# Feed-forward stages: the hidden units computed with the tokens stationary, taken two at a time

## Chip, core and metric

One core of one Trainium2 chip runs the whole program. The metric is the device time of one execution in microseconds (us), as the median of several runs. The profile is a single execution with the hardware profiler on. Engines are named as the profile names them: PE is the matrix engine (PEld its weight load, which overlaps PE), DVE the vector engine, ACT the scalar engine, POOL the GpSimd engine, SP the engine that issues most DMAs.

## What is computed

256 tokens of 1024 channels go through three macaron blocks: feed forward, mixer, feed forward. The kernel runs nine stages in the order f0, m0, f1, f2, m1, f3, f4, m2, f5. The change is in the six feed-forward stages, whose mathematics is this, with 1024 channels, 2816 hidden channels and a residual weight of one half:

```python
def rms_norm_2(x, gain):
    xf = x.astype(jnp.float32)
    y = xf * lax.rsqrt(jnp.mean(xf * xf, axis=-1, keepdims=True) + RMS_EPS)
    return (y * gain.astype(jnp.float32)).astype(x.dtype)

def swiglu_2(x, w_gate, w_up, w_down):
    return (jax.nn.silu(x @ w_gate) * (x @ w_up)) @ w_down

x = x + FFN_RESIDUAL_WEIGHT * swiglu_2(rms_norm_2(x, ffn1_norm[l]),
                                       ffn1_w_gate[l], ffn1_w_up[l], ffn1_w_down[l])
```

## The kernel before

**Precision.** Every float32 factor is split into a high and a low part that PE can multiply fast (type fp32r), and a product is the sum of three: high by high, high by low, low by high. `mm3` (line 176) issues these three matmuls, at lines 177, 178 and 179.

**Weights.** The host lays all weights out as blocks of 128 partitions by 2048 columns in the order of `block_plan`. `W` (line 129) loads a block on first use: two DMAs of 512 KB on SP's queue into `raw` tiles (3 buffers), and for each 512 columns a cast on ACT into `hi` (line 167) and a subtraction on DVE into `lo` (line 169). A block is thus four casts and four subtractions. The pool of split blocks has four buffers, so a block can be split only once the block four before it, or another that is done with, has been used for the last time. The framework orders each engine's instructions by program order and by its own estimate of when they can run; each engine then executes its queue strictly in that order.

**A feed-forward stage** (`ffn`, line 354) has 22 hidden units of 128 channels and two token tiles t = 0, 1 of 128 tokens. The normalized, transposed tokens lie in `xt` as high and low parts.

- `g_as(u, t)` (line 377) computes gate and up of one unit for one token tile with the tokens stationary and the unit's weights moving: for each of 8 slices of the channels one `mm3` with 256 moving columns (128 gate, 128 up). It uses one of the two PSUM banks of `psG`. `glu` (line 363) then reads that bank with three instructions: a tanh `th` on ACT (line 365), `sg` (line 367) and `hu` (line 369) on DVE. The bank is free again when `hu` has run. The result has tokens on partitions, so `g_tr` (line 390) transposes it on PE (line 393) and splits it into `hidh` and `hidl` (lines 182 and 183).
- `g_ws(u)` (line 397) computes a unit for both token tiles with the weights stationary and the tokens moving: per half and channel slice a matmul of 512 columns (line 404) and one of 256 (line 405). Its result needs no transpose.
- `down(u, t)` (line 414) multiplies a unit's hidden channels by its rows of the down weights: six matmuls of 512 columns into two accumulators.

Three units at the head of a stage (four in f4, where `late` is not empty) and two at its tail go through `g_as`, the others through `g_ws`. At the head that lets work on token tile 0 begin while token tile 1 is still being normalized: its last two steps, transposes of the normalized tile at line 224, are hooked into the `g_as` named in line 433, before channel slices 3 and 6, and work on tile 1 comes after. At the tail, `after` (line 278) adds the accumulator of tile 0 to the residual and starts the next stage's norm (`norm_to`, line 227: the scaled tile `xn` is written at line 233, or at line 315 for f4) while PE still works on tile 1. The order at head and tail is written out by hand:

```python
seq = [(u, t) for t in range(NT) for u in range(NA)]     # NA = 3, in f4 4
for i, ut in enumerate(seq):
    hook = finish_at(3, 6) if si and i == NA - 1 else lambda k: None
    g_as(*ut, hook)
    if i > 1:
        g_tr(*seq[i - 2])
...
down(a - 2, 0)                                            # a, b = 20, 21
g_as(a, 0); down(a - 1, 0); g_as(b, 0); g_tr(a, 0); g_as(a, 1); g_tr(b, 0); down(a, 0); down(b, 0)
fin = after(si, 0, acc[0], 0.5)
g_as(b, 1); g_tr(a, 1)
...
down(a - 2, 1); down(a - 1, 1); g_tr(b, 1)
fin()
down(a, 1)
down(b, 1)
```

In f0, `g_as` for token tile 0 runs its three products in three passes over the channels (line 383), since the weights arrive piece by piece.

Of the kernel before, what the change touches and what calls it, by code (L numbers as in the profile page):

```python
# [10 lines left out]
F32R = mybir.dt.float32r  # L11
# [6 lines left out]
P = 128  # L18
D = 1024
KD = 8  # L20
NT = 2
NFU = 22
HALF = 512
EPS = 1e-6
PIECE = 512
# [22 lines left out]
def block_plan(stages):  # L48
    plan = []
    for s in stages:  # L50
        if s[0] == "f":
            for u in range(NFU):
                plan.append(((s, "g", u), 2048))
            for j in range(NFU // 2):
                plan.append(((s, "d", j), 2048))
        elif s == "m0":
            for u in range(4):
                for kh in range(2):
                    plan.append(((s, "p", u, kh), 4 * EV_U))
            for j in range(2):  # L60
                plan.append(((s, "qk", j), 2048))
            for j in range(4):
                plan.append(((s, "o", j), 2048))
        elif s == "m1":
            for kh in range(2):
                plan.append(((s, "a", 0, kh), 4 * IDX_A))
            for u in range(3):
                for kh in range(2):
                    plan.append(((s, "p", u, kh), 2048))
            for j in range(4):  # L70
                plan.append(((s, "o", j), 2048))
# [19 lines left out]
def macaron_kernel(ctx, tc, stages, x, wstream, gains, consts, mconsts, pos, e_small, e_gw, e_on,  # L91
# [95 lines left out]
    def tsl(t):  # L187
        return slice(t * P, (t + 1) * P)
# [165 lines left out]
    def ffn(si):  # L354
        st = stages[si]
        xt = xt_of(si)
        prepare(si + 1)
        fp = ctx2.enter_context(tc.tile_pool(name=f"ffn{si}", bufs=2, reuse_waits="tile"))
        if stages[si:si + 2] == ("f3", "f4"):
            nexts[si + 1]["final"] = load_gain(FINAL_ROW, finp, "fgain")  # L360
        hh, acc, cnt, pend = {}, {}, {(t, n): 0 for t in range(NT) for n in range(2)}, {}

        def glu(ps_g, ps_u, n):
            th = T(fp, 256, "th")
            act(th[:, :n], ps_g, AF.Tanh, scale=0.5)  # L365
            sg = T(fp, 256, "sg")
            V.scalar_tensor_tensor(sg[:, :n], th[:, :n], 1.0, ps_g, op0=ALU.add, op1=ALU.mult)
            hu = T(fp, 256, "hu", bufs=3)
            V.scalar_tensor_tensor(hu[:, :n], sg[:, :n], 0.5, ps_u, op0=ALU.mult, op1=ALU.mult)  # L369
            return hu  # L370

        def hid(u):
            if u not in hh:
                hh[u] = [T(fp, NT * P, f"hid{a}", F32R, bufs=5) for a in "hl"]
            return hh[u]

        def g_as(u, t, hook=lambda k: None):
            wh, wl = W3((st, "g", u), 8, 256)
            ps = bank(psG)
            if si == 0 and t == 0:  # L380
                for i, (a, b) in enumerate(((xt[0], wh), (xt[1], wh), (xt[0], wl))):
                    for k in range(KD):
                        mm(ps[:, :256], lhsT=a[:, k, tsl(t)], rhs=b[:, k], start=i == k == 0, stop=i == 2 and k == 7)  # L383
            else:
                for k in range(KD):
                    hook(k)
                    mm3(ps[:, :256], xt[0][:, k, tsl(t)], xt[1][:, k, tsl(t)], wh[:, k], wl[:, k], k == 0, k == 7)
            pend[u, t] = glu(ps[:, :P], ps[:, P:256], P)

        def g_tr(u, t):  # L390
            hu = pend.pop((u, t))
            pt = bank(psT)
            pe_t(pt[:, :P], hu[:, :P], ident)
            hi, lo = hid(u)
            split_to(hi[:, tsl(t)], lo[:, tsl(t)], pt[:, :P])

        def g_ws(u):
            wh, wl = W3((st, "g", u), 8, 256)
            gu = []
            for m in range(2):  # L400

                ps = bank(psG)
                for k in range(KD):
                    mm(ps, lhsT=wh[:, k, tsl(m)], rhs=xt[2][:, k], start=k == 0, stop=False)  # L404
                    mm(ps[:, :256], lhsT=wl[:, k, tsl(m)], rhs=xt[0][:, k], start=False, stop=k == 7)  # L405
                half = T(fp, 256, "half")
                nc.scalar.copy(half, ps[:, 256:])  # L407
                gu.append(T(fp, 256, f"gu{m}"))
                V.tensor_tensor(gu[m], ps[:, :256], half, op=ALU.add)  # L409
            hu = glu(gu[0], gu[1], 256)  # L410
            hi, lo = hid(u)
            split_to(hi, lo, hu)

        def down(u, t, half=(0, 1)):
            if t not in acc:
                acc[t] = [bank(psA) for _ in range(2)]
            wh, wl = W3((st, "d", u // 2), 2, D)
            a, b = [z[:, tsl(t)] for z in hh[u]]
            for n in half:
                sl = slice(n * HALF, (n + 1) * HALF)  # L420
                mm3(acc[t][n], a, b, wh[:, u % 2, sl], wl[:, u % 2, sl], cnt[t, n] == 0, cnt[t, n] == NFU - 1)
                cnt[t, n] += 1

        if si == 0:
            seq = ((0, 0), (1, 0), (0, 1), (1, 1), (2, 0), (2, 1))
            W((st, "g", 1), (1,))
            W((st, "g", 2), (1, 3), fp)
        else:
            NA = 4 if late else 3
            seq = [(u, t) for t in range(NT) for u in range(NA)]  # L430
        NA = len(seq) // 2
        for i, ut in enumerate(seq):
            hook = finish_at(3, 6) if si and i == NA - 1 else lambda k: None
            g_as(*ut, hook)
            if i > 1:
                g_tr(*seq[i - 2])
        down(0, 0)
        g_tr(*seq[-2])
        down(0, 1)
        g_tr(*seq[-1])  # L440
        a, b = NFU - 2, NFU - 1
        if NA == 4:
            down(1, 0)
            down(1, 1)
        for u in range(NA, a):
            g_ws(u)
            if u == 8:
                with ExitStack() as order:
                    for m in front():
                        order.enter_context(tc.issue_after(m))  # L450
                    while late:
                        late.pop(0)()
                    if st == "f1":
                        rotary_tables()
            down(u - 2, 0)
            if u - 2 < NFU - 4:
                down(u - 2, 1)
        down(a - 2, 0)
        g_as(a, 0); down(a - 1, 0); g_as(b, 0); g_tr(a, 0); g_as(a, 1); g_tr(b, 0); down(a, 0); down(b, 0)
        fin = after(si, 0, acc[0], 0.5)  # L460
        g_as(b, 1); g_tr(a, 1)
        if si + 1 == len(stages):
            for n in range(2):
                for u in (a - 2, a - 1, a, b):
                    if u == a and n == 0:
                        g_tr(b, 1)
                    down(u, 1, (n,))
            after(si, 1, acc[1], 0.5)
            return
        down(a - 2, 1); down(a - 1, 1); g_tr(b, 1)  # L470
        fin()
        down(a, 1)
        down(b, 1)
        tail.append(after(si, 1, acc[1], 0.5))
# [817 lines left out]
    norm_to(0, nexts[0]["gain"], xt_of(0))()  # L1292
    if stages[0][0] == "f":
        with tc.issue_after(last["xn"].ins), tc.issue_after(last["split"].ins):
            W((stages[0], "g", 0), (1,))
    for s in range(2):
        nc.sync.dma_start(h[1][:, s * HALF:(s + 1) * HALF], x[tsl(1), s * HALF:(s + 1) * HALF])
    if stages[0][0] == "f":
# [64 lines left out]
def arrange(inp, stages):  # L1363
# [87 lines left out]
```

## Time and profile before

| | |
|---|---|
| median of 3 runs | 1542.37 us (1540.57 to 1542.55) |
| the profiled execution, its own time | 1545.25 us |
| span of the profile | 1543.5 us |
| mean granted PE clock | 0.993 of full speed |
| PE busy | 1499.1 us, 97% of the span, 8620 matmuls |
| DVE, ACT, POOL busy | 68%, 55%, 7% |
| share of PE on the chain that ended last | 79% |

The chain is followed back from the last instruction through whatever released each step. Matmuls are pipelined, and the profile models their ends, so a row's duration says little of what a matmul costs in a stream; the distance from the start of one to the start of the next does. A number in brackets behind a row of the timeline is the time for which the engine stood idle before it, with the instruction that ended the wait.

### The profile page before, as it was taken

What the parts mean: (1) busy time and instruction counts of PE and PEld (TensorE: products, weight loads), DVE (VectorE), ACT (ScalarE), POOL (GpSimd) and SP (SyncE); (2) the same over time, 40 slices, a digit from 0 to 9 for tenths busy, and PEclk for the clock granted to TensorE, in tenths of its full rate; (3) what the DMA queues carried; (4) which work ended last, traced back from release to release, by engine and by line L of the source; (5) the groups of instructions that cost most, each with busy time, mean ns of one, the idle gap of its engine ahead of it and who ended that gap; (6) DMA issues with size and microseconds to landing.
All of it is one profiled execution on the core that took longest, in us unless ns stands there. A gap on an engine that the chain in (4) does not pass through costs nothing.

```text
span 1543.5 us, 23721 instructions
## 1 busy us (share of the span) xinstructions
PE 1499.1 (97%) x8620; PEld 1308.5 (85%) x8620; DVE 1053.6 (68%) x2282; ACT 851.2 (55%) x1912; POOL 101.3 (7%) x110
## 2 busy tenths in 40 slices
PE   6999998999999999999899999999999999999998
PEld 6888888788888888888688888888888898888887
DVE  6666678766766666668866666767667557776664
ACT  5555464555655555545555555656557566455552
POOL 1000014000000000003100000001002700000000
PEclk9999999999999999999999999999999999999999
DMA  7555554455565555554465655665645424455552
GB/s 246 178 191 185 195 193 134 147 181 191 181 199 169 193 175 196 189 161 131 124 198 185 201 183 161 190 200 186 189 147 186 156 95 150 138 188 191 180 193 94
DMA packets 76549, 268.92 MB, mean 174 GB/s; under 512 B 8832, under 2 KB 10256, under 8 KB 76304
## 3 DMA queue, kind: packets, MB, share of 16 engines
q1 hardware_dynamic: 74160, 260.89, 52.2%
q10 hardware_dynamic: 2272, 6.52, 1.2%
q8 instruction: 67, 1.10, 0.3%
q14 instruction: 50, 0.41, 0.1%
HBM read 266.33 MB, written 1.05 MB: 173 GB/s over the span
## 4 chain that ended last, share of the span: by engine, by line
PE 79%; DVE 8%; DMA 6%; ACT 4%; issue 2%; POOL 1%; SPq 0%; DVEq 0%; ACTq 0%; POOLq 0%
PE g L404 25%; PE g L405 12%; PE acc L179 8%; PE acc L177 8%; PE acc L178 8%; DMA raw<-in_wstream_dram 5%; PE g L177 4%; PE g L179 4%; PE g L178 4%; DVE lo L169 4%; ACT hi L167 2%; PE g L383 1%; PE t L224 1%; DVE xn L233 1%; PE acc L1130 1%
## 5 line engine op out<-in xcount | busy, mean ns | idle before, releaser
L169 DVE TENSOR_TENSOR lo<-raw,hi 128x512 fp32r<-128x512 f32 x994 | 662.1, 694 | 232.2 <-ACT hi L167 228.4
L167 ACT CAST hi<-raw 128x512 fp32r<-128x512 f32 x998 | 565.0, 615 | 276.1 <-DMA raw<-in_wstream_dram 181.4
L404 PE MATMUL g<-xt,hi 128*128 128x512 f32 x1616 | 574.8, 398 | 0.0
L405 PE MATMUL g<-xt,lo 128*128 128x256 f32 x1616 | 453.4, 281 | 0.0
L404 PEld LDWEIGHTS g<-xt,hi 128*128 128x128 f32 x1616 | 303.6, 188 | 74.5 <-DVE gu L409 0.3
L405 PEld LDWEIGHTS g<-xt,lo 128*128 128x128 f32 x1616 | 305.2, 189 | 3.7
L177 PE MATMUL g<-hi,xt 128*128 128x256 f32 (+4 forms) x648 | 204.1, 315 | 7.5 <-DVE hu L369 4.8
L177 PE MATMUL acc<-hi,hidh 128*128 128x512 f32 x528 | 209.8, 397 | 0.7 <-ACT hidh L182 0.7
L178 PE MATMUL acc<-lo,hidh 128*128 128x512 f32 x528 | 207.0, 392 | 0.0
L179 PE MATMUL acc<-hi,hidl 128*128 128x512 f32 x528 | 206.6, 391 | 0.1
L179 PE MATMUL g<-hi,xt 128*128 128x256 f32 (+4 forms) x648 | 199.5, 308 | 0.9 <-DVE xt L183 0.9
L178 PE MATMUL g<-lo,xt 128*128 128x256 f32 (+4 forms) x648 | 199.5, 308 | 0.9 <-DVE lo L169 0.9
L407 ACT COPY half<-g 128x256 f32<-128x256 f32 x202 | 74.6, 369 | 143.0 <-PE g L405 142.8
L177 PEld LDWEIGHTS g<-hi,xt 128*128 128x128 f32 x648 | 124.4, 192 | 13.5 <-ACT th L365 3.4
L409 DVE TENSOR_TENSOR gu<-g,half 128x256 f32<-128x256 f32 x202 | 85.1, 421 | 73.3 <-ACT half L407 73.3
L178 PEld LDWEIGHTS g<-lo,xt 128*128 128x128 f32 x648 | 124.4, 192 | 5.9 <-DVE lo L169 1.3
L179 PEld LDWEIGHTS g<-hi,xt 128*128 128x128 f32 x648 | 124.0, 191 | 5.0 <-DVE xt L183 1.1
L179 PEld LDWEIGHTS acc<-hi,hidl 128*128 128x128 f32 x528 | 99.2, 188 | 23.2 <-DVE hidl L183 1.6
L177 PEld LDWEIGHTS acc<-hi,hidh 128*128 128x128 f32 x528 | 99.2, 188 | 22.8 <-ACT hidh L182 1.0
L178 PEld LDWEIGHTS acc<-lo,hidh 128*128 128x128 f32 x528 | 99.3, 188 | 15.6
L208 POOL TENSOR_TENSOR rs<-ms,nhalf 128x1 f32<-128x1 f32 (+1 forms) x18 | 11.4, 633 | 1057.3 <-DVE ms L218 863.8
L177 PE MATMUL g<-xt,hi 128*128 128x256 f32 x224 | 64.8, 291 | 0.5 <-ACT xt L182 0.5
(293 smaller groups left out, 1507.3 us busy)
## 6 DMA issues: line engine op xcount, KB each, us to landing
raw<-in_wstream_dram SPq DMA_DIRECT2D x472, 512.0 KB, 4.5
raw<-in_wstream_dram SPq DMA_DIRECT2D x16, 388.0 KB, 3.3
gain<-in_gains_dram ACTq DMA_DIRECT2D x8, 512.0 KB, 4.6
raw<-in_wstream_dram SPq DMA_DIRECT2D x4, 360.0 KB, 3.3
raw<-in_wstream_dram SPq DMA_DIRECT2D x4, 324.0 KB, 3.1
h<-in_x_dram SPq DMA_DIRECT2D x4, 256.0 KB, 5.6
mc<-in_mconsts_dram ACTq DMA_DIRECT2D x1, 1024.0 KB, 7.4
out_dram<-h SPq DMA_DIRECT2D x8, 128.0 KB, 1.9
```

Source lines behind the costliest of these rows:

```text
L167: last["hi"] = nc.scalar.copy(hi[:, sl], raw[:, c0:c1])
L169: last["lo"] = eng.tensor_tensor(lo[:, sl], raw[:, c0:c1], hi[:, sl].bitcast(F32), op=ALU.subtract)
L177: mm(o_, lhsT=ah, rhs=bh, start=first, stop=False)
L178: mm(o_, lhsT=ah, rhs=bl, start=False, stop=False)
L179: mm(o_, lhsT=al, rhs=bh, start=False, stop=last)
L224: pe_t(pt[:, k * P:(k + 1) * P], src[:, k * P:(k + 1) * P], ident)
L233: last["xn"] = V.scalar_tensor_tensor(xns[s], h[t][:, sl], rs, gain[:, sl], op0=ALU.mult, op1=ALU.mult)
L383: mm(ps[:, :256], lhsT=a[:, k, tsl(t)], rhs=b[:, k], start=i == k == 0, stop=i == 2 and k == 7)
L404: mm(ps, lhsT=wh[:, k, tsl(m)], rhs=xt[2][:, k], start=k == 0, stop=False)
L405: mm(ps[:, :256], lhsT=wl[:, k, tsl(m)], rhs=xt[0][:, k], start=False, stop=k == 7)
L407: nc.scalar.copy(half, ps[:, 256:])
L409: V.tensor_tensor(gu[m], ps[:, :256], half, op=ALU.add)
```

## The change

Gate and up of two units are computed at once: `g_as` now takes a pair of units, with 512 moving columns in each matmul (256 gate, 256 up), into a whole PSUM bank. Three pairs, 0, 1 and 10, go through it in every stage: units 0 to 3 at the head and 20, 21 at the tail. A pair's weights are two blocks, each with half of the channels for both units. `glu`, the transposes and the split handle 256 columns at a time. At the head, the second half of token tile 1's norm is hooked into the second `g_as` of the stage, before channel slices 2 and 5, and there is no special case for f4. At the tail, the last `g_as` is cut into its two halves of the channels, with the down products of units 20 and 21 for tile 0 between them.

```diff
+PAIRS = (0, 1, 10)
...
             for u in range(NFU):
-                plan.append(((s, "g", u), 2048))
+                if u // 2 not in PAIRS:
+                    plan.append(((s, "g", u), 2048))
+            for p in PAIRS:
+                for kh in range(2):
+                    plan.append(((s, "gp", p, kh), 2048))
...
-                hh[u] = [T(fp, NT * P, f"hid{a}", F32R, bufs=5) for a in "hl"]
-            return hh[u]
+                hh[p] = [T(fp, [2, NT * P], f"hid{a}", F32R, bufs=3) for a in "hl"]
+            return hh[p]
...
+        def g_as(p, t, hook=lambda k: None, parts=(0, 1)):
+
+            if 0 in parts:
+                pend[p, t] = bank(psG)
+            ps = pend[p, t]
+            for kh in parts:
+                wh, wl = W3((st, "gp", p, kh), 4, HALF)
+                if si == 0 and t == 0:
+                    for i, (a, b) in enumerate(((xt[0], wh), (xt[1], wh), (xt[0], wl))):
+                        for k in range(4):
+                            mm(ps, lhsT=a[:, 4 * kh + k, tsl(t)], rhs=b[:, k], start=i == k == kh == 0,
+                               stop=i == 2 and k == 3 and kh == 1)
+                    continue
+                for k in range(4):
+                    kk = 4 * kh + k
+                    hook(kk)
+                    mm3(ps, xt[0][:, kk, tsl(t)], xt[1][:, kk, tsl(t)], wh[:, k], wl[:, k], kk == 0, kk == 7)
+            if 1 in parts:
+                pend[p, t] = glu(ps[:, :256], ps[:, 256:], 256)
+
+        def g_tr(p, t):
+            hu = pend.pop((p, t))
             pt = bank(psT)
-            pe_t(pt[:, :P], hu[:, :P], ident)
-            hi, lo = hid(u)
-            split_to(hi[:, tsl(t)], lo[:, tsl(t)], pt[:, :P])
+            for m in range(2):
+                pe_t(pt[:, tsl(m)], hu[:, tsl(m)], ident)
+            hi, lo = hid(p)
+            split_to(hi[:, :, tsl(t)], lo[:, :, tsl(t)], pt[:, :256].rearrange("p (m n) -> p m n", n=P))
...
+        seq = ((0, 0), (1, 0), (0, 1), (1, 1))
         if si == 0:
-            seq = ((0, 0), (1, 0), (0, 1), (1, 1), (2, 0), (2, 1))
-            W((st, "g", 1), (1,))
-            W((st, "g", 2), (1, 3), fp)
-        else:
-            NA = 4 if late else 3
-            seq = [(u, t) for t in range(NT) for u in range(NA)]
...
+            W((st, "gp", 0, 1), (1,))
+            W((st, "gp", 1, 0), (1, 3), fp)
+        for i, pt_ in enumerate(seq):
+            g_as(*pt_, finish_at(2, 5) if si and i == 1 else lambda k: None)
+            if i:
+                g_tr(*seq[i - 1])
         down(0, 0)
-        g_tr(*seq[-2])
+        down(1, 0)
+        g_tr(*seq[-1])
         down(0, 1)
...
+        c = PAIRS[-1]
+        a, b = 2 * c, 2 * c + 1
+        for u in range(4, a):
             g_ws(u)
...
         down(a - 2, 0)
-        g_as(a, 0); down(a - 1, 0); g_as(b, 0); g_tr(a, 0); g_as(a, 1); g_tr(b, 0); down(a, 0); down(b, 0)
-        fin = after(si, 0, acc[0], 0.5)
-        g_as(b, 1); g_tr(a, 1)
+        g_as(c, 0)
+        down(a - 1, 0)
+        g_as(c, 1, lambda k: g_tr(c, 0) if k == 2 else None, (0,))
         if si + 1 == len(stages):
+            g_as(c, 1, parts=(1,))
+            down(a, 0)
+            down(b, 0)
+            after(si, 0, acc[0], 0.5)
...
-        down(a - 2, 1); down(a - 1, 1); g_tr(b, 1)
+        down(a, 0)
+        down(b, 0)
+        fin = after(si, 0, acc[0], 0.5)
+        g_as(c, 1, parts=(1,))
+        down(a - 2, 1)
+        down(a - 1, 1)
+        g_tr(c, 1)
         fin()
```

## Rows read from the trace of the kernel before

**Rows 1.** The page: span, then busy us, share and instructions by engine.
```profile
span 1543.5 us, 23721 instructions
PE 1499.1 (97%) x8620; PEld 1308.5 (85%) x8620; DVE 1053.6 (68%) x2282; ACT 851.2 (55%) x1912; POOL 101.3 (7%) x110
```
**Rows 2.** The page: the chain that ended last, by engine.
```profile
PE 79%; DVE 8%; DMA 6%; ACT 4%; issue 2%; POOL 1%; SPq 0%; DVEq 0%; ACTq 0%; POOLq 0%
```
**Rows 3.** PE's timeline, f2's head: start us, us, engine line op out<-in; two `g_as`, next transpose.
```profile
495.69 0.28 PE L177 MATMUL g<-hi,xt 128*128 128x256 f32 x1
...
501.44 0.27 PE L224 MATMUL t<-cc,xn 128*128 128x128 f32 x1
```
**Rows 4.** PE's timeline, m2: 24 matmuls of 512 columns, tokens stationary, and the next.
```profile
1175.97 0.39 PE L177 MATMUL g<-hi,xt 128*128 128x512 f32 x1
...
1181.43 0.28 PE L177 MATMUL g<-xt,hi 128*128 128x256 f32 x1
```
**Rows 5.** PE's timeline, f1: the first matmul of a `g_ws` and of the next product.
```profile
421.06 0.39 PE L404 MATMUL g<-xt,hi 128*128 128x512 f32 x1
...
426.70 0.40 PE L177 MATMUL acc<-hi,hidh 128*128 128x512 f32 x1
```
**Rows 6.** PE's timeline, f1: a transpose of `g_tr`, the second matmul after it.
```profile
319.14 0.27 PE L393 MATMUL t<-cc,hu 128*128 128x128 f32 x1
...
319.37 0.28 PE L178 MATMUL g<-lo,xt 128*128 128x256 f32 x1
```
**Rows 7.** PE's timeline: first matmul of the last hooked `g_as`, heads of f1 to f5.
```profile
313.12 0.35 PE L177 MATMUL g<-hi,xt 128*128 128x256 f32 x1 [0.47 <-DVE hu L369]
...
502.79 0.36 PE L177 MATMUL g<-hi,xt 128*128 128x256 f32 x1 [0.53 <-DVE hu L369]
...
786.23 0.36 PE L177 MATMUL g<-hi,xt 128*128 128x256 f32 x1 [3.21 <-DVE hu L369]
...
980.34 0.36 PE L177 MATMUL g<-hi,xt 128*128 128x256 f32 x1 [0.56 <-DVE hu L369]
...
1357.92 0.36 PE L177 MATMUL g<-hi,xt 128*128 128x256 f32 x1 [2.03 <-ACT hi L167]
```
**Rows 8.** DVE's timeline, f5's head: the norm of token tile 1, then `hu`.
```profile
1355.37 1.42 DVE L233 SCALAR_TENSOR_TENSOR xn<-h,rs,gain 128x512 f32<-128x512 f32 x2 [0.45 <-POOL rs L208]
...
1357.50 0.28 DVE L369 SCALAR_TENSOR_TENSOR hu<-sg,g 128x128 f32<-128x128 f32 x1
```
**Rows 9.** Windows, f3's head: length; PE, PEld, DVE, ACT, POOL busy; PEclk; DMA; GB/s.
```profile
777.00:786.20 9.20, 6.03 (x50) 5.78 (x48) 6.45 (x14) 5.44 (x13) 0.93 (x1) 1.00 0.51 160
787.60:791.00 3.40, 3.40 (x18) 3.40 (x17) 1.50 (x3) 0.59 (x1) 0.00 (x0) 0.50 0.83 254
```
**Rows 10.** PE's and DVE's timelines, f3's head: first matmul, norm, last `lo`.
```profile
777.12 0.28 PE L177 MATMUL g<-hi,xt 128*128 128x256 f32 x1
...
783.67 1.42 DVE L233 SCALAR_TENSOR_TENSOR xn<-h,rs,gain 128x512 f32<-128x512 f32 x2 [0.44 <-POOL rs L208]
...
787.13 1.29 DVE L169 TENSOR_TENSOR lo<-raw,hi 128x512 fp32r<-128x512 f32 x2
```
**Rows 11.** PE's and DVE's timelines, f4's head: first matmul, norm of token tile 1.
```profile
970.85 0.28 PE L177 MATMUL g<-hi,xt 128*128 128x256 f32 x1
...
978.59 1.42 DVE L315 SCALAR_TENSOR_TENSOR xn<-xn,rs,gain 128x512 f32<-128x512 f32 x2 [0.62 <-POOL rs L208]
```
**Rows 12.** ACT, DVE and PE at tails: `glu` of f1's last `g_as`; f3's last transpose.
```profile
488.79 0.28 ACT L365 ACTIVATE th<-g 128x128 f32<-128x128 f32 x1 [1.32 <-PE g L179]
...
490.33 0.28 DVE L369 SCALAR_TENSOR_TENSOR hu<-sg,g 128x128 f32<-128x128 f32 x1
...
967.49 0.33 PE L393 MATMUL t<-cc,hu 128*128 128x128 f32 x1 [0.52 <-DVE hu L369]
```
**Rows 13.** ACT's and PE's timelines, f0's head: casts of a late block, the matmuls behind.
```profile
21.54 1.66 ACT L167 CAST hi<-raw 128x512 fp32r<-128x512 f32 x3
...
22.21 2.82 PE L383 MATMUL g<-hi,xt 128*128 128x256 f32 x12 [1.19 <-ACT hi L167]
```

More of the change, by code (lines that the diff above doesn't have):

```diff
@@ L370, in glu @@
             return hu
-        def hid(u):
-            if u not in hh:
-                hh[u] = [T(fp, NT * P, f"hid{a}", F32R, bufs=5) for a in "hl"]
-            return hh[u]
[L377 to L383, printed above, removed]
-            else:
[L385 to L388, printed above, removed]
@@ L390, in g_tr, with hid @@
-        def g_tr(u, t):
-            hu = pend.pop((u, t))
+        def hid(p):
+            if p not in hh:
+                hh[p] = [T(fp, [2, NT * P], f"hid{a}", F32R, bufs=3) for a in "hl"]
[18 more added lines that the diff above has]
+                pend[p, t] = glu(ps[:, :256], ps[:, 256:], 256)
@@ L410, in g_ws @@
             hu = glu(gu[0], gu[1], 256)
-            hi, lo = hid(u)
-            split_to(hi, lo, hu)
+            hi, lo = hid(u // 2)
+            split_to(hi[:, u % 2], lo[:, u % 2], hu)
         def down(u, t, half=(0, 1)):
@@ L417, in down @@
             wh, wl = W3((st, "d", u // 2), 2, D)
-            a, b = [z[:, tsl(t)] for z in hh[u]]
+            a, b = [z[:, u % 2, tsl(t)] for z in hh[u // 2]]
             for n in half:
@@ L422, in down @@
                 cnt[t, n] += 1
+        seq = ((0, 0), (1, 0), (0, 1), (1, 1))
         if si == 0:
-            seq = ((0, 0), (1, 0), (0, 1), (1, 1), (2, 0), (2, 1))
-            W((st, "g", 1), (1,))
-            W((st, "g", 2), (1, 3), fp)
-        else:
-            NA = 4 if late else 3
-            seq = [(u, t) for t in range(NT) for u in range(NA)]
[L431 to L436, printed above, removed]
+            W((st, "gp", 0, 1), (1,))
[4 more added lines that the diff above has]
+                g_tr(*seq[i - 1])
         down(0, 0)
-        g_tr(*seq[-2])
+        down(1, 0)
+        g_tr(*seq[-1])
         down(0, 1)
[L440 to L445, printed above, removed]
+        down(1, 1)
+        c = PAIRS[-1]
+        a, b = 2 * c, 2 * c + 1
+        for u in range(4, a):
             g_ws(u)
@@ L455, in ffn @@
             down(u - 2, 0)
-            if u - 2 < NFU - 4:
-                down(u - 2, 1)
+            down(u - 2, 1)
         down(a - 2, 0)
-        g_as(a, 0); down(a - 1, 0); g_as(b, 0); g_tr(a, 0); g_as(a, 1); g_tr(b, 0); down(a, 0); down(b, 0)
-        fin = after(si, 0, acc[0], 0.5)
-        g_as(b, 1); g_tr(a, 1)
+        g_as(c, 0)
+        down(a - 1, 0)
+        g_as(c, 1, lambda k: g_tr(c, 0) if k == 2 else None, (0,))
         if si + 1 == len(stages):
+            g_as(c, 1, parts=(1,))
+            down(a, 0)
+            down(b, 0)
+            after(si, 0, acc[0], 0.5)
             for n in range(2):
@@ L465, in ffn @@
                     if u == a and n == 0:
-                        g_tr(b, 1)
+                        g_tr(c, 1)
                     down(u, 1, (n,))
@@ L469, in ffn @@
             return
-        down(a - 2, 1); down(a - 1, 1); g_tr(b, 1)
+        down(a, 0)
[4 more added lines that the diff above has]
+        down(a - 1, 1)
+        g_tr(c, 1)
         fin()
@@ L1294, in macaron_kernel @@
         with tc.issue_after(last["xn"].ins), tc.issue_after(last["split"].ins):
-            W((stages[0], "g", 0), (1,))
+            W((stages[0], "gp", 0, 0), (1,))
     for s in range(2):
@@ L1388, in block @@
             return ktiles(np.concatenate([g[:, u * P:(u + 1) * P], up[:, u * P:(u + 1) * P]], axis=1), 8)
+        if kind == "gp":
+            sl, rows = slice(key[2] * 256, (key[2] + 1) * 256), slice(key[3] * 512, (key[3] + 1) * 512)
+            g, up, _ = ffns[s]
+            return ktiles(np.concatenate([g[rows, sl], up[rows, sl]], axis=1), 4)
         if kind == "d":
```

## The prediction

> **What bounds the kernel now.** The page comes first: PE is busy for 1499.1 of the 1543.5 us of the span [rows 1], and 79% of the chain of waits is PE's own work [rows 2]. So what counts is the distance between the starts of successive matmuls, and the places where PE stands still. The profiled execution took 1545.25 us, 2.9 more than the median of the runs shown, 1542.37; the sum is made against the first and then moved to the second. A measurement of this kernel can tell some 0.2%, 3.1 us, from no change, so faster means below 1539.3 and slower above 1545.5.
>
> Next come the timelines of PE, for prices. Two `g_as` in a row, 48 matmuls of 256 columns, take 501.44 - 495.69 = 5.75 us, 2.875 for one and 120 ns a matmul [rows 3]. The same form with 512 columns, tokens stationary and weights moving, occurs in a mixer: 24 matmuls in 1181.43 - 1175.97 = 5.46 us, 227 ns each [rows 4]. A `g_ws` unit takes 426.70 - 421.06 = 5.64 us [rows 5]. From a transpose of `g_tr` to the second matmul after it are 0.23 us; less the matmul between, 0.12, the transpose costs 0.11 [rows 6].
>
> Last come PE's waits at the heads of the feed forwards. In all of f1 to f5 the hooked `g_as`, third in its stage (fourth in f4), begins late, by 0.47, 0.53, 3.21, 0.56 and 2.03 us, 6.8 in all [rows 7]. Four of the waits end with `hu`: the two banks of `psG` are taken, and a bank is free only when `hu` has read it. In the fifth the view names a cast, but `hu` ended at 1357.78, 0.14 us before the matmul [rows 8], so it can as well be what ended the wait, and I count it with them. `hu` is late because the norm of token tile 1 stands ahead of `glu` in DVE's queue [rows 8, 10]. [...]
>
> **The change, part by part.**
>
> *Matmul streams.* The columns per unit stay the same; 24 matmuls of 512 replace 48 of 256. Before, a stage (f4 apart) had five units in `g_as`: 10 x 2.875 + 17 x 5.64 + 10 transposes x 0.11 = 125.7 us. After, it has three pairs: 6 x 5.46 + 16 x 5.64 + 12 x 0.11 = 124.3. That is 1.4 less, 7.0 in five stages. In f4 six units were in `g_as`: 12 x 2.875 + 16 x 5.64 + 12 x 0.11 = 126.1, so 1.8 less. Together -8.8 us, all of it on PE, which is the path.
>
> [...]
>
> *Bank waits.* The third `g_as` of a stage now comes after 48 matmuls of 512, 10.9 us from the start, and needs the bank of a first `g_as` that ended at 5.5. `hu` has 5.5 us for what took it at worst 2.9 + 3.2. In f3 the wait for it ended 9.1 us behind the stage's start (786.23 against 777.12) [rows 7, 10]; it is now wanted at 10.9. I take all 6.8 us off; at the least nothing (first rival). With f3's wait goes its half clock: 18 matmuls took 3.40 us there [rows 9] where at 0.12 they need at most 2.2, so -1.2.
>
> *Norm of token tile 1.* Its transposes are now asked for 5.46 + 6 x 0.227 = 6.8 us after the start. In f4, where they had come after three units, that is 977.7, and the first half of `xn` is out at 978.59 + 0.71 = 979.3 [rows 11]: +1.6, between nothing (if the framework places the transposes later) and 2.3 with the second half. In f3 they are asked for at 783.9, and the half is out at 784.4 [rows 10]: +0.4. In f5 the third `g_as` would have begun at 1355.9, so the stage began at some 1350.1 and asks at 1356.9; the half is out at 1356.1 [rows 7, 8]: nothing, and I take the same for f1 and f2.
>
> *Four blocks instead of three at the head.* A pair needs two blocks, and two pairs run on tile 0, so the fourth block is wanted after 8.2 us and not after 17. The DMAs are the same in number and size (a block is a block), and SP's queue issues them in the same order of use. With the eight hooked transposes (0.9) and f3's 0.4 its first slice is read at start + 9.5 and its last at + 11.8. In f3 the fourth block's last `lo` ended at 788.42, start + 11.3 [rows 10]. It is just ahead; +0.5 for all heads, between 0 and 1.5 in each of five, 7.5.
>
> *Tail.* Between the end of `g_as(c, 0)` and its `g_tr` lie `down(19, 0)` and two channel slices, 12 matmuls of 0.227 = 2.7 us, where it had been 4.2. `glu` of 128 columns took 1.8 us in f1's tail [rows 12]; for 256 columns I add 0.4, by the ratio of sizes an estimate, which still fits. Where the chain is longer PE already waited 0.52 for it [rows 12]. So +0.2 in each of five tails, 1.0, between 0 and 3. Behind that wait stand the down products of tile 0, and behind them `after`, the next stage's norm.
>
> *`glu`, transposes' splits, `hid`.* Fewer and larger instructions on ACT and DVE, off the path; their cover is PE's stream, and without it each would cost its own 0.3 to 0.4 us. Nothing.
>
> *f0's head.* PE waits for the second block's late pieces, cast at 21.54 and used at 22.21 [rows 13]. The matmuls that can run before are as many columns in both kernels (28 of 256, 14 of 512). Nothing, between -1.2 and +1.2, the idle time of that row.
>
> **Sum:** -8.8 - 6.8 - 1.2 + 1.6 + 0.4 + 0.5 + 1.0 = -13.3 us: 1531.9 for a profiled execution, 1529.1 as a median. With the bounds: 1524 to 1539.
>
> **Rivals.**
>
> *The head's wait only moves.* If DVE is the limit there, PE waits as long as before, for the fourth block or the norm. Then the streams and the tail are left, -8.8 + 1.0: a median of 1534.6. For it: at f3's head the norm, `hu` and the subtractions follow each other closely on DVE. Against it: DVE was busy for 6.45 of the 9.2 us before [rows 9], and PE now has 10.9 us of work that needs no bank. 24%.
>
> *A matmul costs by its columns.* If one of 512 cost as much as two of 256 (240 ns), a pair would take 5.75, the sixth unit and two transposes would add 0.3 to each stage, and the waits alone would carry the result: -8.0 + 3.5 + 2.0 = -2.5, 1539.9. [...] 4%.
>
> *The fourth block comes late, and the kernel is slower.* Its buffer is free only when the stage before has ended, and its pieces queue on ACT and DVE behind the norm of tile 1. If its last `lo` landed later than start + 11.8, PE would wait at each of five heads, and a wait as long as f3's would bring its half clock, 1.2 more. Slower begins at 16.4 us above the forecast, 3.3 for each head: 2.1 of wait and 1.2 of clock, a last `lo` at start + 13.9. At waits of 3.2 it is 5 x 4.4 = 22, a median of 1551. For it: the margin in f3 is half a microsecond. Against it: by start + 11.3 the old head had done the same sixteen casts and subtractions and the norm. 5%.
>
> **How the numbers follow.** The forecast with its own bounds near the middle (1524 to 1533) gets 60%, the moved wait 24%, the column price 4%, the late block 5%. A late block by some 2 us without the clock, 1540 to 1545, gets 4%, and a larger gain than summed 3%. Faster: 60 + 24 + 2 (half of the column price) + 3 = 89%; the same: 6%; slower: 5%. The range reaches from 1522 to 1540, so that it holds the moved wait and most of the bounds.
>
> **What would show it.** Right: 24 matmuls of the new `g_as` 5.4 to 5.5 us apart from start to start; no wait of PE for `hu` at the heads of f1, f2, f3 and f5; the clock at 1.00 through f3's head; in f4 a wait of one to two us for `xn` at line 315. Wrong: waits of PE for `lo` at line 169 or a cast at line 167 before the fourth block, a stretch at 0.50 that was not there, waits at the transposes in the tails longer than 0.5 us, or matmuls of 512 columns at 235 ns and more.

## The result, and the profile after the change

The changed kernel takes 1526.6 us (median of 4 runs, 1525.6 to 1529.0); the kernel before, run beside it, 1541.5 (4 runs, 1540.0 to 1542.6). The ratio is 0.9897, with a 95% interval of 0.9882 to 0.9912: 15.9 us faster (the two medians by themselves differ by 14.9). Two later comparisons gave 0.9918 and 0.9903 (below), 12.6 and 15.0 us. The forecast was 1529.1, with a range of 1522 to 1540.

The page of the changed kernel, to set beside [rows 1, 2]: span, busy times, the chain that ended last.

```profile
span 1525.7 us, 21981 instructions
PE 1487.4 (97%) x7846; PEld 1263.3 (83%) x7846; DVE 1044.2 (68%) x2179; ACT 845.0 (55%) x1840; POOL 103.6 (7%) x110
PE 83%; DVE 7%; DMA 5%; ACT 3%; issue 2%; POOL 1%; SPq 0%; DVEq 0%; ACTq 0%; POOLq 0%
```

PE has 774 matmuls fewer and is busy 11.7 us less; its share of the chain rose from 79 to 83%. The bound is the same engine, with fewer gaps. (Line numbers moved: `mm3` is now at 183 to 185, `hi` and `lo` at 173 and 175, `g_tr` at 407, `g_ws` at 418 and 419, `hu` at 375, the norm's transposes at 230, `xn` at 239 and for f4 at 321.)

Price of the new form, PE's timeline in f1's tail: the first matmul of a `g_as` without transposes in it, and the next product, to set beside [rows 3, 4].

```profile
470.14 0.39 PE L183 MATMUL g<-hi,xt 128*128 128x512 f32 x1
...
475.58 0.39 PE L183 MATMUL acc<-hi,hidh 128*128 128x512 f32 x1
```

24 matmuls in 5.44 us, 227 ns each, as the mixer's row had promised. These are of type fp32r; in m1 of the kernel before, four matmuls of 512 columns with plain float32 factors (line 919) and one of fp32r behind them take 1.95 us from the first start to that of the next matmul (755.41 to 757.36, at clock 1.00), some 0.43 us for each of the four.

The view of PE's waits over the whole span: what PE waited for, us in total, times, longest.

```profile
PE t L230 <- DVE xn L321: 1.6, 2, 1.2
...
PE g L418 <- DVE gu L423: 0.9, 2, 0.5
...
PE t L407 <- DVE hu L375: 0.2, 1, 0.2
```

No row with a `g_as` waiting for `hu` is left, where the hooked `g_as` had waited 6.8 us at five heads [rows 7], and no row names a weight block at the heads of f1 to f5. The third row is a tail; the second, two `g_ws` of f1, is new.

Windows at f3's head (length; PE, PEld, DVE, ACT, POOL busy; PEclk; DMA; GB/s), to set beside [rows 9].

```profile
773.38:784.30 10.92, 10.92 (x54) 9.04 (x53) 9.38 (x17) 6.77 (x15) 0.93 (x1) 1.00 0.65 208
784.30:789.00 4.70, 4.70 (x23) 3.86 (x22) 1.42 (x4) 1.26 (x4) 0.00 (x0) 1.00 0.47 187
```

PE is busy all the time, and the clock stays at 1.00. DVE is at 9.38 of 10.92, 86% where it had been 70% [rows 9]: it is harder pressed than before, but PE no longer stands behind it.

DVE's timeline in f3 and f4, and PE's in f4, to set beside [rows 10, 11]: the norm of token tile 1, the fourth block's last `lo`, and the one head at which PE still waits.

```profile
778.01 1.41 DVE L239 SCALAR_TENSOR_TENSOR xn<-h,rs,gain 128x512 f32<-128x512 f32 x2 [0.44 <-POOL rs L214]
...
781.33 1.29 DVE L175 TENSOR_TENSOR lo<-raw,hi 128x512 fp32r<-128x512 f32 x2
...
967.85 1.42 DVE L321 SCALAR_TENSOR_TENSOR xn<-xn,rs,gain 128x512 f32<-128x512 f32 x2 [0.81 <-POOL rs L214]
...
968.74 0.63 PE L230 MATMUL t<-cc,xn 128*128 128x128 f32 x4 [0.43 <-DVE xn L321]
```

The stages begin at 773.38 and 961.36. The norm's last step (`xn`) begins 4.6 and 6.5 us after that, where it had been 6.6 and 7.7; the fourth block is complete at 782.62, 9.2 us after the start of f3.

PE's timeline at the tails of f1 and f3, to set beside [rows 12].

```profile
488.48 0.44 PE L407 MATMUL t<-cc,hu 128*128 128x128 f32 x2 [0.24 <-DVE hu L375]
...
489.85 0.50 PE L183 MATMUL acc<-hi,hidh 128*128 128x512 f32 x1 [0.51 <-ACT hidh L188]
...
957.68 0.63 PE L230 MATMUL t<-cc,xn 128*128 128x128 f32 x4 [1.21 <-DVE xn L321]
```

The waits at the tails, taken as the time by which a matmul starts later than in an unbroken stream (some 0.16 us more each than the idle time in brackets), sum to about 3.1 us over f0 to f4; before it was about 1.6.

Stage by stage, from the first matmul of one stage to that of the next (f0 from the start of the span), in the two profiled executions:

| stage | before | after | difference | forecast (streams, bank wait, clock, norm, block and tail) |
|---|---|---|---|---|
| f0 | 208.11 | 207.03 | -1.1 | -1.2 |
| f1 | 190.96 | 190.33 | -0.6 | -1.6 |
| f2 | 190.20 | 187.50 | -2.7 | -1.6 |
| f3 | 193.73 | 187.98 | -5.8 | -5.1 |
| f4 | 189.72 | 187.85 | -1.9 | -0.5 |
| f5 | 193.48 | 189.86 | -3.6 | -3.3 |
| m0, m1, m2 | 377.24 | 375.18 | -2.1 | 0 |

(The forecast's 0.5 for blocks and 1.0 for tails are spread evenly, 0.1 and 0.2 a stage.) The feed forwards give 15.7 of the 17.7 us between the two profiles; the mixers, which the change does not touch, give 2.1. For those see the last section.

### The profile page after: what moved, and what is told of

It reads as the page before. It is cut to its first block, busy times and chain, and to the rows that moved or that the text cites. A ratio compares the mean times of both kernels' runs of the same rounds, so it can differ in the third digit from the quotient of the medians.

```text
span 1525.7 us, 21981 instructions
## 1 busy us (share of the span) xinstructions
PE 1487.4 (97%) x7846; PEld 1263.3 (83%) x7846; DVE 1044.2 (68%) x2179; ACT 845.0 (55%) x1840; POOL 103.6 (7%) x110
## 4 chain that ended last, share of the span: by engine, by line
PE 83%; DVE 7%; DMA 5%; ACT 3%; issue 2%; POOL 1%; SPq 0%; DVEq 0%; ACTq 0%; POOLq 0%
PE g L418 23%; PE g L419 11%; PE acc L183 9%; PE acc L184 8%; PE acc L185 8%; PE g L185 6%; PE g L183 6%; PE g L184 6%; DMA raw<-in_wstream_dram 3%; DVE lo L175 3%; ACT hi L173 1%; PE g L393 1%; PE t L230 1%; PE acc L1147 1%; PE acc L1122 1%
## 5 line engine op out<-in xcount | busy, mean ns | idle before, releaser
L418 PE MATMUL g<-xt,hi 128*128 128x512 f32 x1536 | 546.4, 398 | 0.9 <-DVE gu L423 0.9
L419 PE MATMUL g<-xt,lo 128*128 128x256 f32 x1536 | 431.1, 281 | 0.0
L418 PEld LDWEIGHTS g<-xt,hi 128*128 128x128 f32 x1536 | 288.6, 188 | 72.0 <-DVE gu L423 1.5
L419 PEld LDWEIGHTS g<-xt,lo 128*128 128x128 f32 x1536 | 290.0, 189 | 3.7
L183 PE MATMUL g<-hi,xt 128*128 128x512 f32 (+3 forms) x456 | 177.1, 388 | 0.7 <-ACT xt L188 0.7
L184 PE MATMUL g<-lo,xt 128*128 128x512 f32 (+3 forms) x456 | 173.2, 380 | 1.3 <-DVE lo L175 1.3
L185 PE MATMUL g<-hi,xt 128*128 128x512 f32 (+3 forms) x456 | 173.3, 380 | 0.7 <-DVE xt L189 0.7
L421 ACT COPY half<-g 128x256 f32<-128x256 f32 x192 | 70.8, 369 | 128.8 <-PE g L419 128.8
L423 DVE TENSOR_TENSOR gu<-g,half 128x256 f32<-128x256 f32 x192 | 80.6, 420 | 65.7 <-ACT half L421 65.7
L185 PEld LDWEIGHTS g<-hi,xt 128*128 128x128 f32 x456 | 86.1, 189 | 15.9 <-DVE xt L189 1.4
L184 PEld LDWEIGHTS g<-lo,xt 128*128 128x128 f32 x456 | 86.4, 189 | 15.1 <-DVE lo L175 1.8
L183 PEld LDWEIGHTS g<-hi,xt 128*128 128x128 f32 x456 | 86.1, 189 | 14.3 <-ACT xt L188 0.9
L214 POOL TENSOR_TENSOR rs<-ms,nhalf 128x1 f32<-128x1 f32 (+1 forms) x18 | 11.8, 658 | 1040.2 <-DVE ms L224 852.2
```

The lines of the kernel that those rows point to most:

```text
L183: mm(o_, lhsT=ah, rhs=bh, start=first, stop=False)
L184: mm(o_, lhsT=ah, rhs=bl, start=False, stop=False)
L185: mm(o_, lhsT=al, rhs=bh, start=False, stop=last)
```

## Experiments

Two questions stood open. Does each part bring what the sum said? And why did the wait at the heads not simply move, which was the largest rival? Ratios are to the kernel before, run on the same chip beside it; 0.001 is 1.5 us.

### One part at a time

**A third bank instead of larger matmuls.** The kernel before, with the later `g_as` of tile 0 in a bank of the accumulators' pool:

```diff
-            ps = bank(psG)
+            ps = bank(psA if si and t == 0 and 2 <= u < NFU - 2 else psG)
```

> The kernel before with one edit: at the heads of f1 to f5 the third (in f4 also the fourth) g_as of token tile 0 accumulates in a bank of the pool psA, which is idle there, so it needs not wait for hu. Everything is computed. Theory (the wait is for the bank of psG): the five waits of 6.8 us at the heads and f3's half clock of 1.2 us go, 1541.5 - 8.0 = 1533.5. Rival (the head is bound by DVE and the wait only moves to the third weight block or the norm of tile 1): PE waits about as long as before, 1539 to 1542.

Measured: 1536.5, ratio 0.9958 [0.9942, 0.9974], 6.5 us. PE's timeline of this kernel at the heads of f3, f4 and f5:

```profile
784.99 0.33 PE L393 MATMUL t<-cc,hu 128*128 128x128 f32 x1 [0.46 <-DVE xt L183]
```
```profile
994.33 0.33 PE L393 MATMUL t<-cc,hu 128*128 128x128 f32 x1 [1.75 <-DVE hu L369]
```
```profile
1352.90 0.33 PE L393 MATMUL t<-cc,hu 128*128 128x128 f32 x1 [1.18 <-DVE xt L183]
```

The waits for a bank are gone, f5's too, which the view of before had put down to a cast, and no stretch of half clock follows at f3's head. But 3.9 us of wait, measured against an unbroken stream, stand at the transposes, the next place that wants what DVE makes. The theory was right in the main; some of the rival is in it.

**The same, with the transposes a step later.**

```diff
-            if i > 1:
-                g_tr(*seq[i - 2])
+            if i > 1 + bool(si):
+                g_tr(*seq[i - 2 - bool(si)])
```

> Computes all that the kernel before does. It is the kernel before with a third bank at the head (as in e1_third_bank) and with each transpose of the head one step later, so that it comes three g_as behind its hu and not two. Theory (in e1 part of the wait for hu came back at the transposes, 3.9 us in f3, f4 and f5): those waits go, the ratio falls from 0.9958 to 0.993 or 0.994 and the time to 8 to 10 us below the kernel before. Rival (the transposes' waits were cover for something else that is late, a split of the next block): the waits at line 393 go, waits for lo or hi appear, and the ratio stays at 0.996.

(Not shown: a fourth buffer for `hu`, and the one transpose more that this puts behind `down(0, 0)`.) Measured: 1544.0, ratio 0.9998 [0.9985, 1.0011]. Nothing is gained at all, less than either theory expected. PE's waits in this kernel:

```profile
PE acc L177 <- ACT hidh L182: 3.1, 4, 1.1
PE g L179 <- DVE xt L183: 3.0, 3, 1.2
PE t L393 <- DVE hidl L183: 2.4, 4, 1.0
...
PE t L393 <- DVE hu L369: 0.5, 1, 0.5
```

Whatever is asked for later on PE, the split parts of token tile 1 (`xt`) and of the hidden channels (`hidh`, `hidl`) are then late. With single units, moving the wait does not remove it.

**Two matmuls of 256 instead of one of 512**, in the changed kernel's `g_as` (but for the first of a group, and f0's token tile 0):

```diff
-                    mm3(ps, xt[0][:, kk, tsl(t)], xt[1][:, kk, tsl(t)], wh[:, k], wl[:, k], kk == 0, kk == 7)
+                    for n in range(2):
+                        sl = slice(n * 256, (n + 1) * 256)
...
+                        mm(ps[:, sl], lhsT=ah, rhs=wl[:, k, sl], start=False, stop=False)
+                        mm(ps[:, sl], lhsT=al, rhs=wh[:, k, sl], start=False, stop=kk == 7 and n == 1)
```

> The changed kernel, with each matmul of 512 columns in g_as cut into two of 256 columns, in the same order and into the same bank (but for the first of a group, and for the first token tile of f0, which keeps its three passes). Everything is computed. Theory (120 ns for 256 columns and 227 for 512): 33 runs of 24 become one of 512 and 46 of 256, 5.75 in place of 5.46 us, +9.5 us in all, 1526.6 + 9.5 = 1536. [...]

Measured: 1534.8, ratio 0.9941 [0.9926, 0.9956]. PE's timeline of the same `g_as` of f1's tail: its first matmul, two of the others, the next product.

```profile
468.92 0.39 PE L403 MATMUL g<-hi,xt 128*128 128x512 f32 x1
...
469.62 0.28 PE L405 MATMUL g<-hi,xt 128*128 128x256 f32 x1
469.74 0.28 PE L406 MATMUL g<-lo,xt 128*128 128x256 f32 x1
...
474.66 0.40 PE L183 MATMUL acc<-hi,hidh 128*128 128x512 f32 x1
```

47 matmuls take 5.74 us against 5.44 for 24, which is 9.9 us in 33 runs. Against the 0.9897 of the changed kernel the cut costs 6.8 us by the times, with some 3 either way from the two intervals, and against the two later comparisons 3.5 and 5.9. The times alone fall short of the theory's 9.5; the rows, and 1.2 to 1.7 a stage in f2 to f5 of the profiles (f2 188.86 against 187.50), speak for it. The rest of the change, without the gain from larger matmuls, is worth 9.1 us, with some 2 either way.

**Head alone, tail alone.** The changed kernel with the tail in single units (`PAIRS = (0, 1)`), and the kernel before with pair 10 at the tail (`PAIRS = (10,)`).

> The changed kernel with pairs 0 and 1 at the head alone; units 20 and 21 at the tail go one by one with 256 columns, in the order of the kernel before. Everything is computed. Theory: four head units in pairs give 0.8 us a stage in streams (1.2 in f4), 5.2 in all, and the head's waits and the half clock, 8.0, go; 0.5 is given back in f4: 1541.5 - 12.7 = 1528.8. Rival (the head's waits were not what was gained, the rest is the tail's): 1541.5 - 5.2 = 1536.

> The changed kernel with the pair (20, 21) at the tail alone; the head is that of the kernel before (three units, in f4 four, one by one). Everything is computed. Theory: two units in a pair give 0.58 us a stage in streams, 3.5 in six; the tail gives 1.0 back; the head's waits stay: 1541.5 - 2.5 = 1539. Rival (the tail is where the gain is): 1532 or less.

Measured: head 1531.2, ratio 0.9915 [0.9898, 0.9932], 13.1 us; tail 1542.2, ratio 0.9985 [0.9970, 0.9999], 2.3 us. By these ratios that is 1528.4 and 1539.2, as the theory had them, and together 15.4 us, with some 2.5 either way on each, against the 15.9, 12.6 and 15.0 of the whole change. In the kernel with the new tail alone the heads wait as before, and f5's wait is here put down to `hu` too; its row in the view of waits:

```profile
PE g L183 <- DVE hu L375: 5.6, 5, 2.0
```

In the kernel with the new head alone f4 waits for the norm as long as the forecast had said:

```profile
969.51 0.63 PE L230 MATMUL t<-cc,xn 128*128 128x128 f32 x4 [1.49 <-DVE xn L321]
```

### Why did the wait not move?

**Narrow `glu` in the changed kernel.** PE's order stays in the program text; on ACT and DVE each pair is handled unit by unit (and `hu` lies in tiles of 128 columns).

```diff
-                pend[p, t] = glu(ps[:, :256], ps[:, 256:], 256)
+                pend[p, t] = [glu(ps[:, m * P:(m + 1) * P], ps[:, 256 + m * P:256 + (m + 1) * P], P) for m in range(2)]
...
-            split_to(hi[:, :, tsl(t)], lo[:, :, tsl(t)], pt[:, :256].rearrange("p (m n) -> p m n", n=P))
+            for m in range(2):
+                split_to(hi[:, m, tsl(t)], lo[:, m, tsl(t)], pt[:, tsl(m)])
```

> Computes all that the changed kernel does, in the same order on PE, but glu, and the split behind the transposes, of each pair run unit by unit (twice as many instructions of 128 columns on ACT and DVE instead of one of 256). Forecast's term (glu and the splits lie off the path, cost nothing): no difference from the changed kernel beside it, within 0.001. Rival (the fewer and larger instructions are why the heads' waits did not come back elsewhere, as they did with a third bank): 0.42 us more of DVE for each pair and tile, waits of PE for hu or hidh at the heads' and tails' transposes of 0.3 to 1 us each, 5 to 10 us in all, ratio higher by 0.003 to 0.006.

The changed kernel itself, beside it:

> The changed kernel, unaltered, beside e8 and e9 on the same chip. Ratio to the kernel before 0.990 to 0.992, as in the two comparisons before.

Measured: narrow 1540.3, ratio 0.9976 [0.9961, 0.9990]; unaltered 1528.5, ratio 0.9903 [0.9878, 0.9928]. The narrow kernel is slower by 0.0073, 11 us, with some 4 either way: the forecast's term would have had no difference, and the rival's 0.006 lies inside. Only 3.7 us of the whole gain are left. The waits of PE, first the narrow kernel, then the unaltered one:

```profile
PE t L407 <- DVE hu L375: 9.6, 11, 1.9
```
```profile
PE t L407 <- DVE hu L375: 1.4, 3, 0.6
```

The 9.6 us stand at the last transposes of the six heads (1.7 in f0, 4.4 in f1 to f5) and at four tails (3.5). At these places few matmuls lie between the end of a `g_as` and its transposes, 12 of 0.227 at the heads. None of the waits is at a `g_as`: with narrow instructions too, no `g_as` waits for a bank. So the wait of before, for a bank, is gone by what changed on PE alone; what narrow instructions bring is waits at other places.

The largest is at f3's head. The timelines of ACT, DVE and PE of the narrow kernel:

```profile
806.30 0.62 ACT L173 CAST hi<-raw 128x512 fp32r<-128x512 f32 x1 [1.38 <-DMA raw<-in_wstream_dram]
...
807.50 0.28 ACT L371 ACTIVATE th<-g 128x128 f32<-128x128 f32 x1
```
```profile
805.71 0.28 DVE L375 SCALAR_TENSOR_TENSOR hu<-sg,g 128x128 f32<-128x128 f32 x1
...
808.62 0.28 DVE L375 SCALAR_TENSOR_TENSOR hu<-sg,g 128x128 f32<-128x128 f32 x1
```
```profile
808.96 0.33 PE L407 MATMUL t<-cc,hu 128*128 128x128 f32 x1 [1.93 <-DVE hu L375]
```

And DVE and PE of the unaltered kernel at the same place:

```profile
798.90 0.41 DVE L375 SCALAR_TENSOR_TENSOR hu<-sg,g 128x256 f32<-128x256 f32 x1
```
```profile
799.49 0.38 PE L407 MATMUL t<-cc,hu 128*128 128x128 f32 x2
```

The first unit's `hu` is early. The second unit's tanh stands in ACT's queue behind a cast that had stood for 1.38 us waiting for its weights, so its `hu` comes 2.9 us after the first, and PE, with down products queued behind it, waits 1.93 us. At the heads of f0, f1, f2 and f4 the second tanh stands behind a cast and the split of the pair before, without such a late block. At the tails it waits for the first unit's `hu` itself. ACT's and PE's timelines at f2's tail:

```profile
681.27 0.28 ACT L371 ACTIVATE th<-g 128x128 f32<-128x128 f32 x1 [0.70 <-DVE hu L375]
```
```profile
682.71 0.33 PE L407 MATMUL t<-cc,hu 128*128 128x128 f32 x1 [0.62 <-DVE hu L375]
```

One wide `glu` has one place in each queue; two narrow ones have two, and run one behind the other: in all 36 `g_as` the second tanh starts only when the first `hu` has ended, in 16 of them with ACT idle until then, and the second `hu` ends 0.95 to 3.6 us after the first. Why this tanh waits for the other unit's `hu` no run shows, and an edit with both tanh ahead was not tried; so the 11 us are the price of these two chained halves and not shown to be that of every narrow form. PE's queue differs too: the framework put a down product between the two transposes at the heads, and transposes of the next norm between them at the tails of f1 and f2. The busy time matters less: two narrow `hu` of 0.28 against one of 0.41 us, 0.15 more for the pair, and that is not where the 11 us come from. Which of the two narrowed parts, `glu` or the split, costs more was not tried alone.

### What was left in the changed kernel

**f4's norm, 1.4 us later:** the hook moves from channel slices 2 and 5 to 4 and 6, in f4 only.

```diff
-            g_as(*pt_, finish_at(2, 5) if si and i == 1 else lambda k: None)
+            g_as(*pt_, finish_at(*((4, 6) if late else (2, 5))) if si and i == 1 else lambda k: None)
```

> Computes all that the changed kernel does; only f4's second half of the norm of token tile 1 is hooked before channel slices 4 and 6 of the second pair, not 2 and 5 (1.4 us later). Theory: PE's wait for xn in f4's head (0.5 us in two profiles, predicted 1.6) goes, and nothing else moves: 0.5 to 1.6 us, not to be told from the changed kernel by the times, within 0.001, but the wait is missing in the trace. Rival (the framework then also places the norm's instructions on DVE later, as it seemed to in e5, where 1.0 us of wait stood at this place): the wait stays at 0.5 us or more.

Measured: 1528.2, ratio 0.9901 [0.9878, 0.9924], against 0.9903 unaltered. PE's timeline in f4's head has no idle time before the norm's transposes any more:

```profile
967.99 0.60 PE L230 MATMUL t<-cc,xn 128*128 128x128 f32 x4
```

So that wait could be moved out of the way alone; f4 lasts 187.6 us against 187.9 beside it. As a gain it is too small to be seen in the times.

**Another order of the tail**, with f4's later hook as well (`ks` names the channel slices that a `g_as` does):

```diff
-        down(a - 2, 0)
         g_as(c, 0)
+        down(a - 2, 0)
         down(a - 1, 0)
-        g_as(c, 1, lambda k: g_tr(c, 0) if k == 2 else None, (0,))
+        g_tr(c, 0)
+        g_as(c, 1, ks=(0, 1))
...
         fin = after(si, 0, acc[0], 0.5)
-        g_as(c, 1, parts=(1,))
+        g_as(c, 1, ks=(2, 3, 4, 5, 6, 7))
```

> Computes all that the changed kernel does. Two of its orders are altered: in the tail, two down products of token tile 0 more, and two channel slices of the last pair, lie behind the end of the pair's first half, so that glu has longer before its transposes and the addition to the residual has more of PE's work before the next stage begins; in f4's head the norm of token tile 1 is hooked before channel slices 4 and 6, not 2 and 5. Theory (waits of the trace are the time lost): f3's tail wait of 1.4 us, f4's head wait of 0.4 to 0.6 and f1's tail waits of about 1 us go, 2.5 us in all less than the changed kernel run beside it, ratio lower by about 0.0016. Rival (each wait only moves to the next place where the same result is wanted): no difference, within 0.001.

> The changed kernel itself, unaltered, beside e5 and e6 on the same chip. Ratio to the kernel before 0.990, as in the first comparison; both theories of e5 are measured against this run. In its profile the waits at the heads are as in the first one (none for hu in f1, f2, f3, f5; 0.4 to 1.7 us for xn in f4), and stretches at half clock may lie elsewhere: if they do, a stage without them should last as long as in the first profile to 0.2 us.

Measured: 1535.8, ratio 0.9953 [0.9937, 0.9968]; unaltered beside it 1529.8, ratio 0.9918 [0.9896, 0.9940]. Both theories missed: the new order is slower, by 0.0035, some 5 us, with 4 either way from the intervals. DVE's timeline in f3's tail and PE's behind it, with this order:

```profile
957.95 0.42 DVE L373 SCALAR_TENSOR_TENSOR sg<-th,g 128x256 f32<-128x256 f32 x1
958.85 1.41 DVE L321 SCALAR_TENSOR_TENSOR xn<-xn,rs,gain 128x512 f32<-128x512 f32 x2 [0.48 <-POOL rs L214]
960.18 0.41 DVE L375 SCALAR_TENSOR_TENSOR hu<-sg,g 128x256 f32<-128x256 f32 x1
```
```profile
960.65 0.44 PE L410 MATMUL t<-cc,hu 128*128 128x128 f32 x2 [1.12 <-DVE hu L375]
```

And DVE's in the changed kernel:

```profile
954.37 0.42 DVE L373 SCALAR_TENSOR_TENSOR sg<-th,g 128x256 f32<-128x256 f32 x1
954.83 0.42 DVE L375 SCALAR_TENSOR_TENSOR hu<-sg,g 128x256 f32<-128x256 f32 x1
...
956.78 1.41 DVE L321 SCALAR_TENSOR_TENSOR xn<-xn,rs,gain 128x512 f32<-128x512 f32 x2 [0.60 <-POOL rs L214]
```

The norm now stands between `sg` and `hu`. PE no longer waits for `xn` at this tail, it waits for `hu`, and after that for `hidh`. In the profiles f2, f3 and f4 last 0.7 to 0.8 us longer each than in the unaltered kernel beside it. f4's head also waits again (0.82 us of idle time for `xn`, with the same hook that removed the wait above). The largest difference is in m0, behind f0's tail: it lasts 101.1 us against 96.1, with PE idle for 1.60 us until `xn` at its start and for 1.94 until `pj` (the copy of the mixer's first products), and 6.8 us at half clock against 3.4; f1 is 2.2 us shorter. Which of this every execution has, one profile doesn't settle.

The unaltered kernel in its two further profiles had the same waits for `xn` as in the first (idle for 0.34 and 0.39 us in f4's head, 1.21 in both at f3's tail). New in them are short waits for `hu` at the last transposes of heads, 0.5 us in f0 in both, 0.2 in f3 and 0.4 in f4 in the one, 0.6 in f5 in the other. A stage without half clock should have lasted as long as in the first profile to 0.2 us; f1 to f4 differ by 0.3 to 0.7 (f1 190.98 against 190.33). So a difference of half a microsecond in one stage is no finding.

## Why the prediction was right

- **Streams, -8.8.** Right. 227 ns for each matmul in the trace; cutting them in two gave back 3.5 to 6.8 us by the times, by which of the three comparisons it is held against, about 8.6 by the stages (1.43 on average in f2 to f5, times six) and 9.9 by the rows. The row of another stage with the same form was the right price.
- **Bank waits, -6.8, and the half clock, -1.2.** All went, as the waits and the windows of f3's head show (the granted clock had been 0.50 for 3.40 us [rows 9] and is 1.00), and the waits stay away with narrow instructions. That the fifth wait was for a bank too, the third bank bears out. The forecast's comparison was short, though: 5.5 us for `hu` against 2.9 + 3.2 = 6.1. What carried the term was the later place: `hu` of f3's first pair ended at 781.42, 8.0 us after the start, and is first wanted at 11.8, where it had been 5.9 (783.02). The stages with the largest waits, f3 and f5, gave 5.8 and 3.6 us, against 5.1 and 3.3 in the sum.
- **`glu` and the splits, nothing: right for wide instructions, without a price for narrow ones.** The forecast put "fewer and larger instructions on ACT and DVE, off the path" at nothing, since PE's stream covers them. The narrow `glu`, with the same products on PE, brings 9.6 us of waits for `hu` at the transposes that follow closely. So the cover is thin there, and the forecast did not look at those places but for the tail's. The rival "the head's wait only moves" (1534.6, 24%) did not come true, but it is what the third-bank kernels show, in part in the first and fully in the second.
- **Norm of tile 1, +1.6 in f4 and +0.4 in f3:** too much; 0.4 of idle time and nothing. The step that failed is the one that left the norm where it had been behind the start of its stage. It moved up by 1.2 us in f4 and 2.0 in f3. In f4 DVE's timeline of before had three instructions of narrow `glu` between the stage's start and `xn`; now the first `glu` comes after it. In f3 DVE's queue had been held by a late cast before the norm's first step, the addition to `h`, whose accumulator had got its last matmul at 776.89:

```profile
779.32 0.69 DVE L169 TENSOR_TENSOR lo<-raw,hi 128x512 fp32r<-128x512 f32 x1 [2.25 <-ACT hi L167]
779.93 1.28 DVE L296 TENSOR_TENSOR h<-acc,h 128x512 f32<-128x512 f32 x2
```

  In the changed kernel the same pair stands 1.9 us nearer to the stage's start, behind 0.33 us of idle time:

```profile
773.66 0.69 DVE L175 TENSOR_TENSOR lo<-raw,hi 128x512 fp32r<-128x512 f32 x1 [0.33 <-ACT hi L173]
774.27 1.28 DVE L302 TENSOR_TENSOR h<-acc,h 128x512 f32<-128x512 f32 x2
```

  With the old tail and the new head the 1.6 was there (1.49 of idle time), so by this one profile it hangs on the tail before it. The cast ahead of f3's norm was to be read before; why it is earlier now was not tried.
- **Fourth block, +0.5:** nothing. It was complete 9.2 us after the start, not 11.3; its first slice was read 8.6 us after the start and its last `lo` at 11.4 (784.75), for which the forecast had 9.5 and 11.8. The margin of the last was 2.1 us, not a half, and the slower rival had no ground.
- **Tail, +1.0:** some 1.5 (3.1 against 1.6 us of waits), half of it in f3, where the norm of f4 is late, and not at the transposes of `hu` alone. A wait of more than 0.5 us at transposes in a tail was named as a sign of being wrong; it showed there (1.21 us).
- **f0, nothing (between -1.2 and +1.2):** its stage fell by 1.1, its share of the streams being 1.4; in the two later profiles of the changed kernel it lasted 205.1 and 206.3, so one profile can't tell it closer.

With the measured sizes the sum is -8.8 - 6.8 - 1.2 + 0.4 + 1.5 = -14.9, which is 1530.4 for a profiled execution. The one after the change took 1527.5; of the difference 2.1 lie in the mixers, which the change does not touch. So what the forecast missed in its own terms (norm, fourth block, tail) comes to 1.6 us. f1 gave less than its share: the two `g_ws` that wait for `gu` take 1.2 us, measured against an unbroken stream.

## What to carry to other kernels

Where PE waits for a result that passes through another engine's queue, giving PE something else to do first often only moves the wait: two kernels here removed a wait for a bank and met it again at the transposes or the split parts. In the changed kernel the first `hu` of f3 is wanted 11.8 us after the stage's start and not 5.9, and that wait went, with narrow instructions too. So list each place where the result is wanted, how far it lies from where the result is made, and what stands ahead of it in the other queues (a norm, a cast that waits for its weights, the other half of the same product), before moving anything on PE. A term that is set to "nothing, hidden" deserves the question what it would cost if it stayed as it was: here 11 us, beside a gain of 16.

## What the runs showed of the hardware that was not expected

Stretches at half clock come and go between executions of the same program, in stages that the change does not touch. Windows over m2's beginning (length; PE, PEld, DVE, ACT, POOL busy; PEclk; DMA; GB/s) in the second profile of the changed kernel, and at the same place in the first:

```profile
1149.67:1159.40 9.73, 7.69 (x41) 6.68 (x40) 5.46 (x17) 5.05 (x12) 0.56 (x1) 1.00 0.52 169
1159.49:1162.90 3.41, 3.41 (x14) 2.92 (x13) 2.44 (x7) 1.90 (x8) 0.86 (x1) 0.50 0.86 268
```
```profile
1149.21:1158.90 9.69, 8.34 (x46) 7.29 (x45) 6.11 (x19) 5.29 (x15) 0.56 (x1) 1.00 0.58 171
1158.90:1162.40 3.50, 3.49 (x19) 2.80 (x18) 2.53 (x8) 2.54 (x8) 0.86 (x1) 1.00 0.75 220
```

In the one PE stood idle 2.0 us before the granted clock fell to 0.50, in the other 1.4, and it did not fall; m2 lasted 189.8 and 186.7 us. The length of the idle time does not tell it alone: at f5's head PE stood idle for 2.03 us in the kernel before and for 1.97 in that with the new tail alone, and only in the second the clock fell, 0.9 us after PE had gone on.

```profile
1357.92:1361.40 3.48, 3.48 (x30) 3.48 (x31) 2.75 (x6) 1.38 (x4) 0.00 (x0) 1.00 0.52 162
```
```profile
1357.65:1361.00 3.35, 3.35 (x18) 3.35 (x18) 2.47 (x5) 1.27 (x3) 0.00 (x0) 0.50 0.60 187
```

Such stretches, of 3.4, 6.8, 10.2 or 13.7 us, stand in m0, m1 or m2 of the other profiles too, each time a little differently. The mixers' 2.1 us in the table are of this kind only in part: before and after, the mixers have 13.7 us at half clock in all, but m1 has 3.4 more after the change (and lasts 1.5 longer), m2 3.4 less (and lasts 2.7 less). So a single profile of this kernel is not good for less than some 3 us, and a stage's own length, with its clock, says more than the span.
